# The modulation gates of a two-layer decoder trunk: summed along features like the shifts, then spread over the partitions through a row in DRAM

## The chip, the cores and the metric

The kernel runs on one core of a Trainium2 chip. The metric is device time in microseconds of the whole program, the median over runs; the version before has a median of 1032.69 us (three runs, 1031.07 to 1036.15).

## The reference

Two layers, batch 1, 256 tokens, model width 1024, float32 throughout. Each layer is a gated feed-forward block, a token mixer, and a second feed-forward block. All three are modulated by vectors that come from a conditioning vector `c`:

```python
c_act = jax.nn.silu(c)                                  # (1, 1024)
for l in range(2):
    mod = (c_act @ w_ada[l] + b_ada[l]).reshape(B, 3, 3, 1024)
    norm_mod = lambda h, j: rms(h) * g_norm[l, j] * (1 + mod[:, j, 1]) + mod[:, j, 0]
    gate     = lambda j: 1 + mod[:, j, 2]
    x = x + 0.5 * gate(0) * swiglu(norm_mod(x, 0), w_up[l, 0], w_down[l, 0])
    x = x +       gate(1) * mixer (norm_mod(x, 1), ...)
    x = x + 0.5 * gate(2) * swiglu(norm_mod(x, 2), w_up[l, 1], w_down[l, 1])
```

`w_ada` is 1024 x 9216 per layer: for each of the three blocks j a third for the shift, one for the scale, one for the gate. The six gates (two layers times three blocks) are what the change is about: each is a vector of 1024 numbers, and the kernel needs it as a tile of 128 partitions x 1024 in which every partition holds the same row, because it multiplies results that have tokens on the partitions and features along the free axis.

## The kernel before

**Matmuls.** Weights arrive from DRAM in units of 128 x 1024 floats (512 KB). `unit` loads one into a tile of the pool `raw` (6 buffers, line 255) and `split` (lines 248 and 249) makes two parts of it: ScalarE rounds it to fp32r (`H`), VectorE subtracts that from the original (`L`). The pool of these pairs has 11 buffers. Each product is three TensorE matmuls (H with the high part of the activations, L with it, H with their low part). A feed-forward block goes over 11 chunks of 256 hidden features: `up_w` (line 467) makes one half of a chunk for all 256 tokens from 4 units, `down` (lines 260 to 262) adds the product of one chunk to the output from 2 units. In steady order a chunk is: `up_w(j, 0)`, `down(j-1, 0)`, `up_w(j, 1)`, `down(j-1, 1)`.

**The modulation.** `w_ada` comes in the same 512 KB units through the same six `raw` buffers. A list `ada_todo` holds 11 stretches in a fixed order; the shift and scale of the very first block are done ahead of it. `ada_step(n)` takes the next n units off the list: after the second half of each chunk (`ADA_FFN`, 5 or fewer), and after each projection of the first layer's mixer (`ADA_MIX`). `ada_until` drains it where a result is needed.

- Shifts and scales (`ada_ss`): the unit is stored with 128 output features on the partitions and the 1024 inputs along the free axis. VectorE multiplies it with `cb`, the activated `c` on every partition, and adds up along the free axis (line 290, with an accumulator). One unit gives one column of 128 features; eight units give a 128 x 8 tile, feature k*128+p at partition p, column k.
- Gates (`ada_gate`): the unit is stored with inputs on the partitions and the 1024 outputs along the free axis. A tile `acc` (128 x 1024, pool `w4`) is set to zero by GpSimd (line 308) and its first row is loaded with the bias (line 309). For each of eight units VectorE adds unit times `cs[:, m]` (the activated `c`, one number a partition) to `acc` (line 313). After the eighth, `split(acc)` makes H and L of it, four TensorE matmuls of 512 columns with a matrix of ones (lines 321 and 322) sum over the partitions and put the sum on all 128 of them, and ScalarE copies the two halves from PSUM to the tile `gate`, with factor and offset 0.5 or 1 (line 323).

**Use of a gate.** `residual` (lines 441 and 442) multiplies a finished output with `gate` on VectorE and adds it to `x`. The tile `gate` has one buffer for block 1 and one shared by blocks 0 and 2; `gate_free` keeps a new gate from being begun before the last reader of its buffer has been emitted.

**Order.** All DMAs are issued by SyncE (SP), one after the other. The order of each engine's instructions is fixed when the program is built: a scheduler goes through the emitted instructions by priority (the order of emission) and lets a later one pass an earlier one that isn't ready by its model; on the chip each engine then keeps that order.

Of the kernel before, what the change touches and what calls it, by code (L numbers as in the profile page):

```python
# [9 lines left out]
F32 = mybir.dt.float32  # L10
# [3 lines left out]
AF = mybir.ActivationFunctionType  # L14
# [5 lines left out]
D = 1024  # L20
# [37 lines left out]
def ada_units():  # L58
    keys = []
    for l in range(DEPTH):  # L60
        for j in range(3):
            keys += [("ss", l, j, k, v) for k in range(KT) for v in range(2)]
            keys += [("gt", l, j, m) for m in range(KT)]
    return {k: i for i, k in enumerate(keys)}


# [7 lines left out]
def _offsets(sizes):  # L74
# [5 lines left out]


PAR, N_PAR = _offsets(
    [("c", KT), ("lam", 4 * DEPTH)]
    + [(f"{n}{l}{j}", KT) for l in range(DEPTH) for j in range(3) for n in ("bs", "bc", "gn")]
    + [(f"{n}{l}", k) for l in range(DEPTH)
       for n, k in (("cw", 16), ("cb", 4), ("br", 4), ("bi", 4), ("gm", 8), ("wf", 4 * KT))]
)
# [4 lines left out]


@with_exitstack
def trunk_kernel(ctx: ExitStack, tc: tile.TileContext, x, c, wst, ada, par, cst, row, bgate, wg, out):
    nc = tc.nc
    pool = lambda name, bufs, **k: ctx.enter_context(tc.tile_pool(name=name, bufs=bufs, **k))
    const = pool("const", 1)
# [11 lines left out]
    def W4(shape, dt=F32, name="w4"):  # L110
        return w4.tile(shape, dt, tag="w4", name=name)
# [48 lines left out]
    def P(name):  # L160
        o, n = PAR[name]
        return p_sb[:, o:o + n]
# [12 lines left out]
    RS = 0.5 * NEWTON ** 3  # L175


    cs = const.tile([128, KT], F32, name="cs")
    for n in range(2):
        q = slice(n * 512, (n + 1) * 512)  # L180
        o = PT([128, 512], name="pc")
        T.matmul(o, lhsT=one_row, rhs=c_row[:, q], start=True, stop=True)
        A.activation(cb[:, q], o, AF.Silu)
    A.activation(cs, P("c"), AF.Silu)

    V.tensor_scalar(out=P("gn00"), in0=P("gn00"), scalar1=RS, scalar2=None, op0=ALU.mult)
    V.scalar_tensor_tensor(out=P("bc00"), in0=P("bc00"), scalar=1.0, in1=P("gn00"), op0=ALU.add, op1=ALU.mult)
# [56 lines left out]
    def split(raw):  # L244
        h = hlp.tile([128, 1024], F32R, tag="H", name="H")
        lo = hlp.tile([128, 1024], F32R, tag="L", name="L")
        with held("A"):
            A.copy(h, raw)  # L248
        V.tensor_tensor(out=lo, in0=raw, in1=h.bitcast(F32), op=ALU.subtract)  # L249
        return h, lo  # L250
# [26 lines left out]

    ss_t = {}
    G_t, S_t, gate_t = {}, {}, {}
    acc_t = {}  # L280

    def ada_ss(l, j, k, v):
        if (k, v) == (0, 0):
            ss_t[l, j] = const.tile([128, 2, KT], F32, name=f"ss{l}{j}")
            G_t[l, j] = const.tile([128, KT], F32, name=f"G{l}{j}")
            S_t[l, j] = const.tile([128, KT], F32, name=f"S{l}{j}")
        raw = rawp.tile([128, D], F32, tag="raw", name="raw")
        S.dma_start(out=raw, in_=ada[A_UNITS["ss", l, j, k, v]])
        st = ss_t[l, j]
        V.scalar_tensor_tensor(out=raw, in0=raw, scalar=1.0, in1=cb,  # L290
                               op0=ALU.mult, op1=ALU.mult, accum_out=st[:, v, k:k + 1])
        first = (l, j) == (0, 0)
        if v == 1 and (first or k == KT - 1):
            q = slice(k, k + 1) if first else slice(0, KT)
            V.tensor_tensor(out=S_t[l, j][:, q], in0=st[:, 0, q], in1=P(f"bs{l}{j}")[:, q], op=ALU.add)
            if first:
                V.tensor_scalar(out=G_t[l, j][:, q], in0=st[:, 1, q], scalar1=P(f"gn{l}{j}")[:, q],
                                scalar2=P(f"bc{l}{j}")[:, q], op0=ALU.mult, op1=ALU.add)
                return
            V.scalar_tensor_tensor(out=G_t[l, j][:, q], in0=st[:, 1, q], scalar=1.0, in1=P(f"bc{l}{j}")[:, q],  # L300
                                   op0=ALU.add, op1=ALU.add)
            V.scalar_tensor_tensor(out=G_t[l, j][:, q], in0=G_t[l, j][:, q], scalar=RS, in1=P(f"gn{l}{j}")[:, q],
                                   op0=ALU.mult, op1=ALU.mult)

    def ada_gate(l, j, m):
        if m == 0:
            acc_t[l, j] = W4([128, D], name="acc")
            nc.gpsimd.memset(acc_t[l, j], 0.0)
            S.dma_start(out=acc_t[l, j][0:1, :], in_=bgate[l * 3 + j:l * 3 + j + 1, :])
        raw = rawp.tile([128, D], F32, tag="raw", name="raw")  # L310
        S.dma_start(out=raw, in_=ada[A_UNITS["gt", l, j, m]])
        acc = acc_t[l, j]
        V.scalar_tensor_tensor(out=acc, in0=raw, scalar=cs[:, m:m + 1], in1=acc, op0=ALU.mult, op1=ALU.add)
        if m == KT - 1:
            g = const.tile([128, D], F32, name=f"gate{j % 2}", tag=f"gate{j % 2}")
            f = 1.0 if j == 1 else 0.5
            h, lo = split(acc)
            for n in range(2):
                q = slice(n * 512, (n + 1) * 512)
                o = PT([128, 512], name="pg")  # L320
                T.matmul(o, lhsT=ones_r, rhs=h[:, q], start=True, stop=False)
                T.matmul(o, lhsT=ones_r, rhs=lo[:, q], start=False, stop=True)
                A.activation(g[:, n * 512:(n + 1) * 512], o, AF.Copy, scale=f, bias=f)
            gate_t[l, j] = g


# [635 lines left out]
def _pack(inp):  # L962
    f = lambda n: np.asarray(inp[n])
    up, dn, wi, wo, wa = f("w_ffn_up"), f("w_ffn_down"), f("w_in"), f("w_out"), f("w_ada")
    wst = np.empty((len(W_UNITS), 128, 1024), up.dtype)
    for key, i in W_UNITS.items():
        if key[0] == "up":
            _, l, s, j, h = key
            a = up[l, s].reshape(KT, 128, 2, FF)[2 * h:2 * h + 2, :, :, j * CH:(j + 1) * CH]
            wst[i] = a.transpose(1, 0, 2, 3).reshape(128, 1024)  # L970
        elif key[0] == "dn":
            _, l, s, j, h = key
            wst[i] = dn[l, s, j * CH + h * 128:j * CH + (h + 1) * 128]
        elif key[0] == "in":
            _, l, g, h = key
            a = np.concatenate([wi[l][:, lo:hi] for lo, hi in GROUP_COLS[g]], axis=1)
            wst[i] = a.reshape(KT, 128, 512)[2 * h:2 * h + 2].transpose(1, 0, 2).reshape(128, 1024)
        else:
            _, l, m = key
            wst[i] = wo[l, m * 128:(m + 1) * 128]  # L980
    ada = np.empty((len(A_UNITS), 128, 1024), wa.dtype)
    for key, i in A_UNITS.items():
        if key[0] == "ss":
            _, l, j, k, v = key
            ada[i] = wa[l].reshape(D, 3, 3, KT, 128)[:, j, v, k, :].T
        else:
            _, l, j, m = key
            ada[i] = wa[l].reshape(128, KT, 3, 3, D)[:, m, j, 2, :]

    par = np.zeros((128, N_PAR), np.float32)  # L990

    def put(name, a):
        o, n = PAR[name]
        par[:, o:o + n] = a

    cols = lambda v: v.reshape(-1, 128).T
    put("c", f("c").reshape(128, KT))
    put("lam", cols(f("lru_lambda")))
    ba = f("b_ada").reshape(DEPTH, 3, 3, D)
    for l in range(DEPTH):  # L1000
        for j in range(3):
            put(f"bs{l}{j}", cols(ba[l, j, 0]))
            put(f"bc{l}{j}", cols(ba[l, j, 1]))
            put(f"gn{l}{j}", cols(f("g_norm")[l, j]))
        put(f"cw{l}", cols(f("conv_w")[l]))
        put(f"cb{l}", cols(f("conv_b")[l]))
        put(f"br{l}", cols(f("b_rgate")[l]))
        put(f"bi{l}", cols(f("b_igate")[l]))
        put(f"gm{l}", cols(f("g_mix_out")[l]))
        put(f"wf{l}", wi[l][:, 2560:2564].reshape(KT, 128, 4).transpose(1, 0, 2).reshape(128, 4 * KT))  # L1010

    row = np.zeros((1, N_ROW), np.float32)
    for l in range(DEPTH):
        for n, a in (("bf", f("b_fgate")[l]), ("gqk", f("g_qk")[l].reshape(-1))):
            o, k = ROW[f"{n}{l}"]
            row[0, o:o + k] = a

    i = np.arange(128)
    le = i[:, None] <= i[None, :]
    consts = {  # L1020
        "ident": np.eye(128), "ntri": -1.0 * ~(i[:, None] < i[None, :]),
        "trif": le, "msb": np.where(i[:, None] < i[None, :], 0.0, -1e30),
        "mfx": np.where(i[None, :] <= i[:, None], 0.0, -1e30), "fold": i[:, None] % 4 == np.arange(4)[None, :],
    }
    cst = np.concatenate([consts[n] for n in CST], axis=1).astype(np.float32)

    wg = np.zeros((DEPTH, 128, 2, 4, 128), np.float32)
    for gi, n in enumerate(("w_rgate", "w_igate")):
        w = f(n).reshape(DEPTH, 4, 2, HD, HD)
        for b in range(2):  # L1030
            wg[:, b * HD:(b + 1) * HD, gi, :, b * HD:(b + 1) * HD] = w[:, :, b].transpose(0, 2, 1, 3)
    return {
        "x": f("x").reshape(SEQ, D), "c": f("c").reshape(1, D), "wst": wst, "ada": ada, "par": par, "cst": cst,
        "row": row, "bgate": np.ascontiguousarray(ba[:, :, 2].reshape(DEPTH * 3, D)), "wg": wg,
    }


# [15 lines left out]
```

## Time and profile before

| | |
|---|---|
| median of the runs | 1032.69 us |
| the profiled execution | 1031.17 us, span 1029.4 us |
| TensorE matmuls | 994.3 us busy, 97% of the span |
| VectorE | 759.9 us, 74% |
| ScalarE | 538.1 us, 52% |
| GpSimd | 53.3 us, 5% |
| DMA | 248.10 MB, mean 241 GB/s |
| mean granted TensorE clock | 0.994 |

The time of the profiled execution holds its span and 1.8 us around it. In the profile a row of a group reads: line, engine, operation, output <- inputs, shapes, count; then the busy time of the group in us and the mean of one instruction in ns; then how long the engine had been idle just before, and what ended that. PE is TensorE, PEld its weight loads, DVE VectorE, ACT ScalarE, POOL GpSimd, SPq the issuing of DMAs by SyncE. Matmuls overlap, so a matmul's own duration is longer than its step to the next one.

### The profile page before, as it was taken

How to read it: one execution, taken by the hardware profiler on the slowest of the kernel's cores; microseconds unless marked ns; L12 is line 12 of the kernel's file. 1: busy time of each engine (PE TensorE's matmuls, PEld its weight loads, DVE VectorE, ACT ScalarE, POOL GpSimd, SP SyncE). 2: the span in 40 equal slices, each digit the busy share in tenths (PEclk: the TensorE clock that was granted, in tenths of full speed). 3: DMA queues.
4: the chain of work that ended last, by engine and by line, in shares of the span. 5: the costliest groups of instructions: out<-in, count | busy, mean ns of one | idle time of the engine just before them, and what ended most of it. 6: DMA issues, size and time to landing. Idle time of an engine off the chain costs nothing.

```text
span 1029.4 us, 15807 instructions
## 1 busy us (share of the span) xinstructions
PE 994.3 (97%) x6038; PEld 871.8 (85%) x6038; DVE 759.9 (74%) x1107; ACT 538.1 (52%) x855; POOL 53.3 (5%) x108
## 2 busy tenths in 40 slices
PE   5999999989999899999999999999999989999998
PEld 4999999868787799999878999997777778999996
DVE  7988978769786898888569888665677559745452
ACT  5373534458774444354454455455679454635340
POOL 1000000120011200000020000001100120000000
PEclk9999999989999999999999999999999999999999
DMA  8989998757473699999539999853542328755511
GB/s 307 362 308 315 332 332 312 268 207 255 155 252 117 241 362 336 335 331 328 194 124 340 342 334 335 304 191 137 173 175 83 103 86 324 266 203 171 198 63 41
DMA packets 68922, 248.10 MB, mean 241 GB/s; under 512 B 7783, under 2 KB 8423, under 8 KB 68846
## 3 DMA queue, kind: packets, MB, share of 16 engines
q1 hardware_dynamic: 68846, 247.10, 68.2%
q8 instruction: 47, 0.77, 0.3%
q14 instruction: 29, 0.24, 0.1%
HBM read 246.02 MB, written 1.05 MB: 240 GB/s over the span
## 4 chain that ended last, share of the span: by engine, by line
PE 83%; ACT 6%; POOL 4%; DVE 3%; issue 2%; DMA 1%; SPq 0%; DVEq 0%; POOLq 0%; ACTq 0%
PE up L467 38%; PE dn L260 8%; PE dn L262 8%; PE dn L261 8%; PE up L271 5%; PE pj L271 5%; PE up L273 3%; PE pj L273 2%; ACT H L248 2%; POOL na L360 1%; PE wo L260 1%; PE wo L261 1%; PE wo L262 1%; POOL ny L361 1%; PE tp L415 1%
## 5 line engine op out<-in xcount | busy, mean ns | idle before, releaser
L249 DVE TENSOR_TENSOR L<-raw,H 128x1024 fp32r<-128x1024 f32 x320 | 380.5, 1221 | 72.6 <-ACT H L248 71.8
L248 ACT CAST H<-raw 128x1024 fp32r<-128x1024 f32 x320 | 328.1, 1051 | 84.5 <-PE up L467 35.0
L467 PE MATMUL up<-hTh,H 128*128 128x256 f32 x1088 | 211.0, 282 | 3.7 <-ACT H L248 3.7
L467 PE MATMUL up<-hTl,H 128*128 128x256 f32 x1088 | 211.9, 283 | 0.0
L467 PE MATMUL up<-hTh,L 128*128 128x256 f32 x1088 | 211.3, 282 | 0.0
L467 PEld LDWEIGHTS up<-hTh,H 128*128 128x128 f32 x1088 | 169.2, 189 | 9.9 <-ACT H L248 4.1
L467 PEld LDWEIGHTS up<-hTl,H 128*128 128x128 f32 x1088 | 165.1, 189 | 0.0
L467 PEld LDWEIGHTS up<-hTh,L 128*128 128x128 f32 x1088 | 164.4, 189 | 0.0
L459 ACT ACTIVATE sg<-up 128x256 f32<-128x256 f32 x88 | 33.7, 383 | 223.9 <-PE up L467 183.6
L260 PE MATMUL dn<-H,gh 128*128 128x512 f32 x352 | 141.1, 401 | 1.6 <-ACT gh L532 1.6
L262 PE MATMUL dn<-H,gl 128*128 128x512 f32 x352 | 140.0, 399 | 0.0
L261 PE MATMUL dn<-L,gh 128*128 128x512 f32 x352 | 139.7, 397 | 0.0
L290 DVE SCALAR_TENSOR_TENSOR raw<-raw,cb 128x1024 f32<-128x1024 f32 x96 | 114.0, 1220 | 2.1 <-DMA raw<-in_ada 2.1
L262 PEld LDWEIGHTS dn<-H,gl 128*128 128x128 f32 x352 | 66.6, 189 | 15.8 <-DVE gl L533 0.5
L260 PEld LDWEIGHTS dn<-H,gh 128*128 128x128 f32 x352 | 66.7, 189 | 15.2 <-ACT gh L532 3.0
L261 PEld LDWEIGHTS dn<-L,gh 128*128 128x128 f32 x352 | 66.9, 190 | 12.8
L516 DVE TENSOR_TENSOR sg<-sg,up 128x256 f32<-128x256 f32 x68 | 28.5, 419 | 66.0 <-ACT sg L459 65.7
L271 PE MATMUL pj<-H,hTh 128*128 128x512 f32 x160 | 66.2, 414 | 0.0
L273 PE MATMUL pj<-H,hTl 128*128 128x512 f32 x160 | 65.9, 412 | 0.0
L271 PE MATMUL up<-H,hTh 128*128 128x512 f32 x160 | 64.2, 401 | 0.4 <-DVE hTh L428 0.4
L271 PE MATMUL pj<-L,hTh 128*128 128x512 f32 x160 | 64.5, 403 | 0.0
L271 PE MATMUL up<-L,hTh 128*128 128x512 f32 x160 | 63.1, 395 | 0.0
(249 smaller groups left out, 1101.5 us busy)
## 6 DMA issues: line engine op xcount, KB each, us to landing
raw<-in_wst SPq DMA_DIRECT2D x320, 512.0 KB, 5.2
raw<-in_ada SPq DMA_DIRECT2D x144, 512.0 KB, 5.3
x<-in_x SPq DMA_DIRECT2D x2, 512.0 KB, 3.7
wgt<-in_wg SPq DMA_DIRECT2D x2, 512.0 KB
out_x<-x SPq DMA_DIRECT2D x4, 256.0 KB
once<-in_cst SPq DMA_DIRECT2D x1, 192.0 KB
p_sb<-in_par SPq DMA_DIRECT2D x1, 148.0 KB, 5.4
r_sb<-in_row SPq DMA_DIRECT2D x1, 132.0 KB, 6.1
```

Of the source, the lines that this page charges most:

```text
L248: A.copy(h, raw)
L249: V.tensor_tensor(out=lo, in0=raw, in1=h.bitcast(F32), op=ALU.subtract)
L260: T.matmul(o, lhsT=xh, rhs=wh, start=first, stop=False)
L261: T.matmul(o, lhsT=xh, rhs=wl, start=False, stop=False)
L262: return T.matmul(o, lhsT=xl, rhs=wh, start=False, stop=last)
L271: T.matmul(o, lhsT=hh[:, k, :], rhs=part, start=k == 0 and i == 0, stop=False)
L273: mul = T.matmul(o, lhsT=hl[:, k, :], rhs=w(k)[0], start=False, stop=k == KT - 1)
L290: V.scalar_tensor_tensor(out=raw, in0=raw, scalar=1.0, in1=cb, op0=ALU.mult, op1=ALU.mult, accum_out=st[:, v, k:k + 1])
L360: E.tensor_scalar(out=a, in0=y, scalar1=v, scalar2=y, op0=ALU.mult, op1=ALU.mult)
L459: used.append(A.activation(*a, **k))
L467: return T.matmul(o[:, v], lhsT=w[:, q:q + 128], rhs=(hTh, hTl)[h][:, :, k, :], start=opens, stop=True, skip_group_check=True)
L516: V.tensor_tensor(out=sg, in0=sg, in1=o[:, 1], op=ALU.mult)
```

## The change

The gates are computed as the shifts are. The gate units are stored in the layout of the shift units, and VectorE makes one column of 128 features from each, with `cb`. After the eighth unit two small VectorE instructions on 128 x 8 add the bias (now a part of the table of parameters `par`, `bg`) and apply `(1 + v) * f`. Then SP stores the 128 x 8 tile to a row of 1024 floats in DRAM, feature k*128+p at its place, and loads that row into all 128 partitions of `gate`. `acc`, its zeroing, the bias load, `cs`, the split, the four matmuls and the two copies go. The tiles `ss` of the shifts and scales now share two buffers.

```diff
-    + [(f"{n}{l}{j}", KT) ... for n in ("bs", "bc", "gn")]
+    + [(f"{n}{l}{j}", KT) ... for n in ("bs", "bc", "bg", "gn")]
...
-    A.activation(cs, P("c"), AF.Silu)
...
-            ss_t[l, j] = const.tile([128, 2, KT], F32, name=f"ss{l}{j}")
+            ss_t[l, j] = const.tile([128, 2, KT], F32, name=f"ss{l}{j}", tag=f"ss{(3 * l + j) % 2}")
...
-    def ada_gate(l, j, m):
-        if m == 0:
-            acc_t[l, j] = W4([128, D], name="acc")
-            nc.gpsimd.memset(acc_t[l, j], 0.0)
-            S.dma_start(out=acc_t[l, j][0:1, :], in_=bgate[l * 3 + j:l * 3 + j + 1, :])
+    rows = pool("rows", 2, space=bass.MemoryType.DRAM)
+
+    def ada_gate(l, j, k):
+
+        if k == 0:
+            gt_t[l, j] = const.tile([128, KT], F32, name=f"gt{l}{j}", tag=f"gt{j % 2}")
         raw = rawp.tile([128, D], F32, tag="raw", name="raw")
-        S.dma_start(out=raw, in_=ada[A_UNITS["gt", l, j, m]])
-        acc = acc_t[l, j]
-        V.scalar_tensor_tensor(out=acc, in0=raw, scalar=cs[:, m:m + 1], in1=acc, op0=ALU.mult, op1=ALU.add)
-        if m == KT - 1:
+        S.dma_start(out=raw, in_=ada[A_UNITS["gt", l, j, k]])
+        col = gt_t[l, j]
+        V.scalar_tensor_tensor(out=raw, in0=raw, scalar=1.0, in1=cb, op0=ALU.mult, op1=ALU.mult,
+                               accum_out=col[:, k:k + 1])
+        if k == KT - 1:
+            f = 1.0 if j == 1 else 0.5
+            V.tensor_tensor(out=col, in0=col, in1=P(f"bg{l}{j}"), op=ALU.add)
+            V.tensor_scalar(out=col, in0=col, scalar1=1.0, scalar2=f, op0=ALU.add, op1=ALU.mult)
+            r = rows.tile([1, D], F32, tag="row", name="row")
+            S.dma_start(out=r.rearrange("o (k p) -> p (o k)", p=128), in_=col)
             g = const.tile([128, D], F32, name=f"gate{j % 2}", tag=f"gate{j % 2}")
-            f = 1.0 if j == 1 else 0.5
-            h, lo = split(acc)
-            for n in range(2):
-                q = slice(n * 512, (n + 1) * 512)
-                o = PT([128, 512], name="pg")
-                T.matmul(o, lhsT=ones_r, rhs=h[:, q], start=True, stop=False)
-                T.matmul(o, lhsT=ones_r, rhs=lo[:, q], start=False, stop=True)
-                A.activation(g[:, n * 512:(n + 1) * 512], o, AF.Copy, scale=f, bias=f)
+            S.dma_start(out=g, in_=r.broadcast_to([128, D]))
             gate_t[l, j] = g
```

More of the change, by code (lines that the diff above doesn't have):

```diff
@@ L62, in ada_units @@
             keys += [("ss", l, j, k, v) for k in range(KT) for v in range(2)]
-            keys += [("gt", l, j, m) for m in range(KT)]
+            keys += [("gt", l, j, k) for k in range(KT)]
     return {k: i for i, k in enumerate(keys)}
@@ L82 @@
 PAR, N_PAR = _offsets(
-    [("c", KT), ("lam", 4 * DEPTH)]
-    + [(f"{n}{l}{j}", KT) for l in range(DEPTH) for j in range(3) for n in ("bs", "bc", "gn")]
+    [("lam", 4 * DEPTH)]
+    + [(f"{n}{l}{j}", KT) for l in range(DEPTH) for j in range(3) for n in ("bs", "bc", "bg", "gn")]
     + [(f"{n}{l}", k) for l in range(DEPTH)
@@ L94, in trunk_kernel @@
 @with_exitstack
-def trunk_kernel(ctx: ExitStack, tc: tile.TileContext, x, c, wst, ada, par, cst, row, bgate, wg, out):
+def trunk_kernel(ctx: ExitStack, tc: tile.TileContext, x, c, wst, ada, par, cst, row, wg, out):
     nc = tc.nc
@@ L175, in trunk_kernel @@
     RS = 0.5 * NEWTON ** 3
-    cs = const.tile([128, KT], F32, name="cs")
     for n in range(2):
@@ L279, in trunk_kernel @@
     G_t, S_t, gate_t = {}, {}, {}
-    acc_t = {}
+    gt_t = {}
     def ada_ss(l, j, k, v):
         if (k, v) == (0, 0):
-            ss_t[l, j] = const.tile([128, 2, KT], F32, name=f"ss{l}{j}")
+            ss_t[l, j] = const.tile([128, 2, KT], F32, name=f"ss{l}{j}", tag=f"ss{(3 * l + j) % 2}")
             G_t[l, j] = const.tile([128, KT], F32, name=f"G{l}{j}")
@@ L986, in _pack @@
         else:
-            _, l, j, m = key
-            ada[i] = wa[l].reshape(128, KT, 3, 3, D)[:, m, j, 2, :]
+            _, l, j, k = key
+            ada[i] = wa[l].reshape(D, 3, 3, KT, 128)[:, j, 2, k, :].T
     par = np.zeros((128, N_PAR), np.float32)
@@ L996, in _pack @@
     cols = lambda v: v.reshape(-1, 128).T
-    put("c", f("c").reshape(128, KT))
     put("lam", cols(f("lru_lambda")))
@@ L1003, in _pack @@
             put(f"bc{l}{j}", cols(ba[l, j, 1]))
+            put(f"bg{l}{j}", cols(ba[l, j, 2]))
             put(f"gn{l}{j}", cols(f("g_norm")[l, j]))
@@ L1033, in _pack @@
         "x": f("x").reshape(SEQ, D), "c": f("c").reshape(1, D), "wst": wst, "ada": ada, "par": par, "cst": cst,
-        "row": row, "bgate": np.ascontiguousarray(ba[:, :, 2].reshape(DEPTH * 3, D)), "wg": wg,
+        "row": row, "wg": wg,
     }
```

## The prediction

> **What bounds the kernel now.** I read first how the engines are filled over stretches of time. Columns after the stretch: its length, then busy us of PE, PEld, DVE, ACT and POOL with counts, the granted PE clock, the DMA share and GB/s.
>
> ```profile
> 100.00:150.00 50.00, 50.00 (x358) 46.95 (x357) 42.53 (x55) 22.49 (x33) 0.00 (x0) 1.00 0.94 333
> 200.00:250.00 50.00, 45.16 (x195) 35.69 (x194) 40.10 (x58) 34.48 (x52) 9.71 (x11) 0.93 0.67 231
> 400.00:475.00 75.00, 75.00 (x531) 70.17 (x530) 61.17 (x89) 34.57 (x47) 0.00 (x0) 1.00 0.94 335
> 520.00:600.00 80.00, 78.36 (x475) 69.23 (x474) 71.28 (x90) 41.65 (x65) 5.47 (x8) 1.00 0.80 283
> ```
>
> In the feed-forward blocks (first and third row) TensorE has no gap at all: 50.00 of 50 and 75.00 of 75 us. But the DMA engines are 94% busy there and VectorE 85% (42.53 of 50): two others are close behind. Only around the mixer (second row) does TensorE idle, 4.8 us of 50, and its clock falls with it to 0.93.
>
> Next, in the timeline of PE, what the old spreading of a gate costs there; this is the first gate (the last two rows are for later).
>
> ```profile
> 114.36 0.39 PE L321 MATMUL pg<-H,ones_r 128*128 128x512 f32 x1
> 114.59 0.39 PE L322 MATMUL pg<-L,ones_r 128*128 128x512 f32 x1
> 114.82 0.39 PE L321 MATMUL pg<-H,ones_r 128*128 128x512 f32 x1
> 115.05 0.39 PE L322 MATMUL pg<-L,ones_r 128*128 128x512 f32 x1
> 115.28 0.39 PE L260 MATMUL dn<-H,gh 128*128 128x512 f32 x1
> ...
> 118.08 0.40 PE L467 MATMUL up<-hTh,H 128*128 128x256 f32 x2
> ...
> 125.16 0.40 PE L260 MATMUL dn<-H,gh 128*128 128x512 f32 x1
> ```
>
> Each matmul lasts 0.39 us, but the next begins 0.23 us after it: the four hold TensorE for 115.28 - 114.36 = 0.92 us, with real work right behind. The group of these matmuls over the whole program:
>
> ```profile
> L322 PE MATMUL pg<-L,ones_r x12: 392/392/581, 114.6 to 880.0; 128*128 128x512 f32 x12
> its engine sat idle before it (us, times) until:
> who waited for it (us, times):
> ```
>
> Twelve here and as many for line 321. Under neither of the two headings stands an entry: TensorE never waited for the split, and nobody for the sum. What they cost is their place in the queue of the engine that bounds the kernel.
>
> **The change part by part.**
>
> *TensorE.* 24 matmuls go, at a step of 0.23 us: 24 x 0.23 = 5.5 us; nothing is added. With no idle time around them, in five of six gates everything behind moves up by that. In the second gate, which is made in the mixer, TensorE is 45.16 of 50 us busy, so a tenth of its 0.9 us may be lost in a gap. I take 5.5 us.
>
> *VectorE, ScalarE, GpSimd.* The old tile `acc`, and then the shift's form of the sum, which the new gate takes over:
>
> ```profile
> L313 DVE SCALAR_TENSOR_TENSOR acc<-raw,cs,acc x48: 1275/1284/1287, 79.1 to 868.5; 128x1024 f32<-128x1024 f32 x48
> L308 POOL MEMSET acc<- x6: 951/951/977, 8.7 to 843.3; 128x1024 f32 x6
> L309 SPq DMA_DIRECT2D acc<-in_bgate x6: 243/244/281, 68.8 to 844.3; - x6
> L248 ACT CAST H<-acc x6: 1047/1048/1051, 105.2 to 869.8; 128x1024 fp32r<-128x1024 f32 x6
> L249 DVE TENSOR_TENSOR L<-acc,H x6: 1218/1226/1227, 106.3 to 870.9; 128x1024 fp32r<-128x1024 f32 x6
> its engine sat idle before it (us, times) until:
>   DVE acc L313: 26.8, 5
> ```
>
> ```profile
> L290 DVE SCALAR_TENSOR_TENSOR raw<-raw,cb x96: 1211/1220/1227, 11.7 to 662.1; 128x1024 f32<-128x1024 f32 x96
> L290 DVE DVE_READ_ACCUMULATOR raw<-raw,cb x96: 78/83/89, 12.9 to 663.2; 128x1 f32 x96
> ```
>
> A gate costs VectorE 8 x (1.220 + 0.083 - 1.284) = +0.15 us for the sums, -1.23 us for the low part, and two new instructions on 128 x 8. Those lie between the 0.083 us of a 128 x 1 read and the 1.22 us of 128 x 1024; at their size nearer the first, I take 0.2 us each. That is -0.7 us a gate, 4 us in all. ScalarE loses six casts of 1.05 us, twelve copies and, worth more, the 26.8 us in which it stood before the cast of `acc` with everything else queued behind. None of that was on TensorE's path, so it is costed at nothing; at most it moves weights forward. GpSimd's six clearings (0.95 us) are off the path too. A pair H and L of the eleven is no longer taken by `acc`.
>
> *The way through DRAM.* A gate must be ready when the residual multiplies with it:
>
> ```profile
> L441 DVE TENSOR_TENSOR tmp<-dn,gate x16: 682/690/694, 197.6 to 1024.9; 128x512 f32<-128x512 f32 x16
> L323 ACT ACTIVATE gate<-pg x12: 592/601/612, 115.8 to 880.5; 128x512 f32<-128x512 f32 x12
> ```
>
> The first gate is made at 115.8 us and first used at 197.6. Eighty us cover two DMAs many times over, so their latency is free; without that cover it would be the store's and the load's landing, some 10 us a gate. What isn't free is the queue they stand in. All loads of weights go through SP:
>
> ```profile
> 101.38 7.98 SPq L255 DMA_DIRECT2D raw<-in_wst  x6
> 110.55 6.95 SPq L288 DMA_DIRECT2D raw<-in_ada  x5
> ```
>
> The store waits for the second small VectorE instruction, 0.4 us after the sum that also frees the next `raw` buffer, so at this point SP would have had little else to issue. The load back waits until the store has landed, and behind it wait loads of weights that could start when a `raw` buffer comes free. How long a landing takes:
>
> ```profile
> q1 hardware_dynamic: 68846, 247.10, 68.2%
> ...
> raw<-in_ada SPq DMA_DIRECT2D x144, 512.0 KB, 5.3
> ...
> r_sb<-in_row SPq DMA_DIRECT2D x1, 132.0 KB, 6.1
> ```
>
> ```profile
> SPq L1049 <- DMA out_x<-x: 1.6, 2, 1.4
> ```
>
> With other loads ahead of it, 5.3 us for 512 KB and 6.1 us for a short row spread to all partitions, which is just the kind of load that is added; for a store with nothing ahead, SP waited 1.4 us at the very end. The store is peculiar: feature k*128+p of partition p lies 512 bytes from its next, so 128 x 8 values are 1024 separate pieces of 4 bytes, 64 for each of 16 DMA engines. No row shows such a transfer. Bounds: nothing beyond an ordinary landing; or every piece as dear as the mean packet of the profile, 0.682 x 16 x 1029.4 us / 68846 = 163 ns, which is 64 x 0.163 = 10.4 us. A mean packet carries 3.6 KB (247.10 MB / 68846), a thousand times a piece, so I take a value near the low end, 1 us.
>
> The Trainium skill speaks against the change here: in "DMA: Bandwidth & Descriptors", Rules for kernel authors, a strided last dimension lowers to one descriptor per element and should be rearranged; under Specifications, below 512 bytes the engine does a read-modify-write. It gives no price per piece; by it the time would lie towards the upper bound, and the sum below would end as in the rival that is slower.
>
> So SP may stand for up to 5.3 + 1 = 6.3 us a gate, less what the scheduler has put between store and load. The load adds 512 KB at 333 GB/s, 1.6 us. What hides this is the lead of the weights over TensorE; in the timeline of DVE after the first gate:
>
> ```profile
> 101.27 3.92 DVE L313 SCALAR_TENSOR_TENSOR acc<-raw,cs,acc 128x1024 f32<-128x1024 f32 x3
> ...
> 109.29 4.63 DVE L249 TENSOR_TENSOR L<-raw,H 128x1024 fp32r<-128x1024 f32 x4
> ...
> 118.68 1.22 DVE L249 TENSOR_TENSOR L<-raw,H 128x1024 fp32r<-128x1024 f32 x1
> ```
>
> The four units at 109.29 are the next chunk's. The first is ready at 110.5 and used at 118.08: a lead of 7.6 us. The unit at 118.68 is the second of a `down`, ready at 119.9, used at 125.16: 5.3 us, the smallest. A stand of 6.3 us that begins with the queue still holding several loads eats the lead, but hardly more. I cost it at 0; the ends are -2 us (a pair and VectorE time more for the weights) and +10.4 us a gate (dear pieces, below). Lost lead can be regained: VectorE has 15% of the time free.
>
> *The rest.* `par` grows by 40 columns, 20 KB or 0.06 us at 333 GB/s; the activation for `cs` goes; `ss` shares two buffers, each read out before the next but one begins. Nothing for these.
>
> Sum: -5.5 us. The profiled execution's 1031.17 us (its span 1029.4 and 1.8 around it) would become 1025.7. The median of the runs is 1.5 us higher, 1032.69, so 1027.2 us.
>
> **The rivals.**
>
> *The gain is given back.* DMA (94%) and VectorE (85%) take over as soon as TensorE is faster, or the lead that is lost at a gate is paid for by small waits. For it: a chunk of 17 us has 16 us of DMA, and the added load makes 17.6 in one chunk. Against it: TensorE has not one gap there now. It leaves 1029 to 1033, I say 1031.
>
> *Slower: SP stands longer than the lead.* Place: the four gates in stretches with full DMA (first, third, fourth, fifth). Price: stand less 5.3 us, each time. It decides from 5.3 us on; slower by 0.5% (5.2 us) it gets when the four lose 5.5 + 5.2 = 10.7 us, so at a stand of 8.0 us. At the upper bound, 5.3 + 10.4 = 15.7 us, TensorE loses 4 x 10.4 = 42 us: 1069. At half that price a piece, 4 x 5.2 - 5.5 = +15: 1048, which I name. For it: 1024 pieces; against it: their few bytes, and loads still on their way.
>
> *More is gained.* ScalarE's 26.8 us and the free pair let weights come earlier where TensorE does wait, in the 1.6 us idle of 520 to 600 and the 4.8 of 200 to 250: up to 4 us more, 1023.
>
> **How the numbers follow.** The forecast has 0.50, its own range 1024.5 to 1029.5; given back 0.25; slower 0.13; more 0.12. A measurement can tell about 0.5%, 5.2 us, from no change: faster is below 1027.5. That holds for two thirds of the forecast (its small errors lean to the gain) and for "more": 0.34 + 0.12 = 0.46. Same: 0.16 and 0.22 of "given back", 0.38. Slower: 0.03 and 0.13, 0.16. The range 1022 to 1037 leaves out the dear part of "slower" and a little of "more".
>
> **What would show it.** Right: no row `pg`; `dn` 0.23 us after `up` at that place; PE busy about 5 us lower and still 50.00 of 50 in the first stretch; SP's wait for the store under 6 us. Wrong: waits of PE or PEld for `H` or `L` within 20 us of a gate, SP waiting over 8 us on the row's store, a clock under 1.00 in the feed-forward blocks.

## The result and the profile after

The changed kernel takes 1072.87 us (median of four runs, 1069.66 to 1074.85) against 1033.09 us beside it: 1.038 times as long, interval 1.034 to 1.042. The forecast was 1027.2 us.

The page of the changed kernel: busy time of the engines, and the two new DMAs in the list of issues (KB each, median us from issue to landing, which is when the transfer is reported complete).

```profile
PE 1005.9 (94%) x6014; PEld 876.5 (82%) x6014; DVE 750.4 (70%) x1161; ACT 530.3 (49%) x836; POOL 49.8 (5%) x102
...
gate<-row SPq DMA_DIRECT2D x6, 512.0 KB, 6.6
```

```profile
row<-gt SPq DMA_DIRECT2D x6, 4.0 KB, 13.1
```

The 24 matmuls are gone (6014 in place of 6038), and yet PE is busy 11.6 us longer. The span is 1073.1 us, so PE is idle 67.2 us, where it was 1029.4 - 994.3 = 35.1 before. Idle 32.1 more and busy 11.6 more make the 43.7 us between the two spans. And the store of 4 KB, the smallest transfer of the change, takes 13.1 us to land. That figure is the median of the two stores, of six, whose landing the trace could tell; SP issues the load that waits for the store 10.9 to 14.0 us after it, with a median of 12.2.

What each engine does in the 20 us that follow each of the six stores (PE, PEld, DVE, ACT, POOL; then PE clock, DMA share, GB/s):

```profile
101.70:121.70 20.00, 18.55 (x130) 16.85 (x128) 6.71 (x9) 3.89 (x6) 0.00 (x0) 1.00 0.53 148
238.30:258.30 20.00, 12.44 (x56) 9.61 (x54) 8.96 (x11) 8.34 (x12) 0.00 (x0) 0.90 0.72 151
383.30:403.30 20.00, 17.40 (x113) 15.90 (x113) 5.91 (x9) 4.11 (x7) 0.00 (x0) 0.94 0.53 148
580.70:600.70 20.00, 16.19 (x107) 14.75 (x106) 5.82 (x8) 4.50 (x7) 0.00 (x0) 0.96 0.64 115
624.40:644.40 20.00, 10.21 (x65) 9.03 (x64) 5.32 (x8) 2.50 (x3) 0.00 (x0) 0.80 0.55 125
907.70:927.70 20.00, 20.00 (x141) 18.36 (x139) 6.96 (x9) 4.78 (x7) 0.00 (x0) 1.00 0.48 130
```

The kernel before, in the 20 us after its second and its fifth gate's sum:

```profile
232.00:252.00 20.00, 20.00 (x90) 16.21 (x89) 18.86 (x29) 17.61 (x26) 0.00 (x0) 1.00 0.84 288
605.00:625.00 20.00, 20.00 (x136) 18.38 (x136) 15.91 (x24) 9.04 (x14) 0.00 (x0) 1.00 0.98 339
```

Where 288 to 362 GB/s flowed at the six places before, 115 to 151 do; VectorE works 5 to 9 us of 20 because it has no data. TensorE falls from full work to 10.2 of 20 us at the fifth store and to 12.4 at the second, the one in the mixer. After the sixth it still lives on its lead, and pays a little later: in the timeline of PE it waits 3.75 us, and then its matmuls step by 0.42 to 0.59 us, soon by a steady 0.43, in place of 0.23 (the first two rows), while the granted clock is 0.50 (the row of a stretch below).

```profile
927.16 0.39 PE L259 MATMUL dn<-L,gh 128*128 128x512 f32 x1
927.39 0.40 PE L260 MATMUL dn<-H,gl 128*128 128x512 f32 x1
931.54 0.79 PE L258 MATMUL dn<-H,gh 128*128 128x512 f32 x1 [3.75 <-ACT gh L518]
932.13 0.63 PE L259 MATMUL dn<-L,gh 128*128 128x512 f32 x1
932.58 0.79 PE L260 MATMUL dn<-H,gl 128*128 128x512 f32 x1
933.17 0.63 PE L258 MATMUL dn<-H,gh 128*128 128x512 f32 x1
933.59 0.63 PE L259 MATMUL dn<-L,gh 128*128 128x512 f32 x1
934.02 0.63 PE L260 MATMUL dn<-H,gl 128*128 128x512 f32 x1
```

```profile
934.00:936.50 2.50, 2.50 (x12) 2.38 (x11) 2.50 (x3) 1.89 (x3) 0.00 (x0) 0.50 0.84 316
```

That is how PE can be busier with fewer matmuls: the mean granted clock fell from 0.994 to 0.975.

The first store closer, as SP issues it and as the DMA engines then move data (last two columns: share, GB/s):

```profile
101.72 0.39 SPq L319 DMA_DIRECT2D row<-gt  x1
102.16 1.05 SPq L253 DMA_DIRECT2D raw<-in_wst  x2
112.65 0.33 SPq L321 DMA_DIRECT2D gate<-row  x1
113.03 1.92 SPq L253 DMA_DIRECT2D raw<-in_wst  x3
```

```profile
101.00:103.00 2.00, 2.00 (x19) 2.00 (x18) 1.93 (x7) 0.00 (x0) 0.00 (x0) 1.00 0.20 30
103.00:105.00 2.00, 2.00 (x15) 1.83 (x14) 1.22 (x3) 0.66 (x2) 0.00 (x0) 1.00 0.11 1
105.00:107.00 2.00, 2.00 (x11) 1.63 (x10) 1.48 (x3) 0.96 (x2) 0.00 (x0) 1.00 0.18 14
107.00:109.00 2.00, 2.00 (x20) 2.00 (x19) 0.25 (x1) 0.00 (x0) 0.00 (x0) 1.00 0.32 37
109.00:111.00 2.00, 2.00 (x20) 2.00 (x19) 0.00 (x0) 0.00 (x0) 0.00 (x0) 1.00 0.25 23
111.00:113.00 2.00, 2.00 (x18) 1.92 (x17) 0.00 (x0) 0.00 (x0) 0.00 (x0) 1.00 0.60 29
```

Two things happen. SP stands from 103.2 to 112.65 us before the load of the gate. In the list of SP's waits (us in total, times, longest) this wait has 11.1 us a time, for the four stores for which the trace names it:

```profile
SPq L321 <- DMA row<-gt: 44.5, 4, 12.4
```

And the two loads of weights that it had issued right behind the store don't come either: from 101 to 113 us 1 to 37 GB/s flow. ScalarE, in its timeline, waits for just these:

```profile
116.41 1.05 ACT L246 CAST H<-raw 128x1024 fp32r<-128x1024 f32 x1 [10.45 <-DMA raw<-in_wst]
```

The trace also records each packet that the DMA engines move. The 1024 pieces themselves are quick: by this record they take 7 to 9 ns each, and the last of them has passed 1.6 us after the first store's issue. The packets of 4096 bytes behind them, which carry weights, are slow: up to 6.9 us each in this kernel, where their median is 0.159 us. So the time goes by between the pieces' passing and the store's landing, and not in handling one piece after another.

### The profile page after: what moved, and what is told of

Its sections match the earlier page's. It is cut to its first block, busy times and chain, and to the rows that moved or that the text cites. A ratio compares the mean times of both kernels' runs of the same rounds, so it can differ in the third digit from the quotient of the medians.

```text
span 1073.1 us, 15747 instructions
## 1 busy us (share of the span) xinstructions
PE 1005.9 (94%) x6014; PEld 876.5 (82%) x6014; DVE 750.4 (70%) x1161; ACT 530.3 (49%) x836; POOL 49.8 (5%) x102
## 4 chain that ended last, share of the span: by engine, by line
PE 55%; issue 23%; DMA 7%; ACT 6%; DVE 5%; POOL 4%; SPq 0%; POOLq 0%; ACTq 0%; DVEq 0%
PE up L465 23%; PE dn L258 5%; PE dn L259 5%; PE dn L260 5%; DMA raw<-in_wst 5%; PE pj L269 4%; PE up L269 3%; ACT H L246 2%; PE pj L271 2%; PE up L271 2%; POOL na L358 1%; DVE raw L312 1%; DMA row<-gt 1%; DVE L L247 1%; PE wo L258 1%
## 5 line engine op out<-in xcount | busy, mean ns | idle before, releaser
L465 PE MATMUL up<-hTh,H 128*128 128x256 f32 x1088 | 213.4, 284 | 18.8 <-ACT H L246 18.8
```

The lines of the kernel that those rows point to most:

```text
L465: return T.matmul(o[:, v], lhsT=w[:, q:q + 128], rhs=(hTh, hTl)[h][:, :, k, :], start=opens, stop=True, skip_group_check=True)
```

## The experiments

Two theories. P: the 1024 pieces of the store hold up the DMA engines, whoever waits for it. Q: the price is SP standing in front of the load of the gate, with the weights queued behind. Where pieces are concerned two more, N and C, come below.

**The store without anyone waiting for it.**

```diff
-            S.dma_start(out=g, in_=r.broadcast_to([128, D]))
+            S.dma_start(out=g, in_=c.broadcast_to([128, D]))
```

> Left out: the gate tile is loaded from the vector c, not from the stored row, so the numbers of the gates are not those of the reference; the store of 1024 pieces stays, but nothing waits for it. Theory P (the pieces themselves hold up the DMA engines for some 12 us, whoever waits): SP issues its loads at once, but they land some 12 us late all the same, about 1060 to 1073 us. Theory Q (the price is SP standing before the load of the gate, with the weights queued behind it): without the wait at most 1032 us. Near 1050 both hold a part.

1056.87 us, 1.024 times the time before (1.022 to 1.025): between the two. The wait accounts for 1072.87 - 1056.87 = 16 us; the larger part stays although SP is free. In the 16 us lies one thing more: as nothing ties the load of the gate to the store now, it is issued elsewhere, the first at 91.50 us, ahead of the store at 100.72. The 20 us after the first store:

```profile
100.70:120.70 20.00, 18.52 (x131) 16.86 (x130) 8.12 (x11) 6.27 (x8) 0.00 (x0) 1.00 0.77 183
```

183 GB/s, with six loads of weights issued at once behind the store.

**Neither store nor wait.**

```diff
-            S.dma_start(out=r.rearrange("o (k p) -> p (o k)", p=128), in_=col)
-            S.dma_start(out=g, in_=r.broadcast_to([128, D]))
+            S.dma_start(out=g, in_=c.broadcast_to([128, D]))
```

> Left out: the store; the gate tile is loaded from the vector c, so its numbers are not those of the reference. What is left is the change without its way through DRAM, with the same 512 KB load. Both theories: the sum of the prediction without any stand of SP, 1027 us (1024 to 1031). If it is over 1035, something else than the store made the change slow (the sums, the load of the gate, the new order of the engines).

1024.78 us, 0.9925 of the time before (0.991 to 0.994). So the sums in the new form, the bias, and a 512 KB load into all partitions cost nothing and the gain is there; the store alone, with nobody waiting, costs 1056.87 - 1024.78 = 32 us. That is the larger part of what the change lost, and it is theory P's.

**Pieces of 32 bytes.** The host packs the gate's units so that column k of partition p is feature 8p + k.

```diff
-            S.dma_start(out=r.rearrange("o (k p) -> p (o k)", p=128), in_=col)
+            S.dma_start(out=r.rearrange("o (p k) -> p (o k)", p=128), in_=col)
...
-            ada[i] = wa[l].reshape(D, 3, 3, KT, 128)[:, j, 2, k, :].T
+            ada[i] = wa[l].reshape(D, 3, 3, 128, KT)[:, j, 2, :, k].T
...
-            put(f"bg{l}{j}", cols(ba[l, j, 2]))
+            put(f"bg{l}{j}", ba[l, j, 2].reshape(128, KT))
```

> The gate units are packed so that partition p holds features 8p to 8p+7: the store becomes 128 pieces of 32 bytes in place of 1024 of 4, with the same wait and the same load. Theory P: an eighth of the pieces, 1.6 us in place of 13; the store lands some 5 us after its issue, within the lead of the weights, 1027 to 1034 us. Theory Q in the form that any round trip through DRAM behind full queues is too long: little changes, over 1050 us.

1024.45 us, 0.9922 of the time before (0.9903 to 0.994): the version that beats both kernels, with the same wait and the same round trip through DRAM. The store's row and its landing, then the first and the second gate's 20 us:

```profile
L319 SPq DMA_DIRECT2D row<-gt x6: 326/327/330, 101.9 to 864.1; - x6
...
DMA to landing us min/median/max: 1.4/1.4/3.0
```

```profile
101.90:121.90 20.00, 20.00 (x146) 18.79 (x145) 15.54 (x23) 7.74 (x11) 0.00 (x0) 1.00 0.88 332
232.00:252.00 20.00, 19.89 (x87) 15.44 (x86) 17.69 (x26) 17.21 (x28) 0.00 (x0) 1.00 0.90 292
```

Landed after 1.4 us in place of 13.1, and faster as a whole than either theory said; TensorE has no gap at the first gate and none worth the name at the second. Q in the form that any round trip is too long has fallen.

**Both DMAs on GpSimd's queue**, with the 1024 pieces as they were.

```diff
-            S.dma_start(out=r.rearrange("o (k p) -> p (o k)", p=128), in_=col)
+            nc.gpsimd.dma_start(out=r.rearrange("o (k p) -> p (o k)", p=128), in_=col)
...
-            S.dma_start(out=g, in_=r.broadcast_to([128, D]))
+            nc.gpsimd.dma_start(out=g, in_=r.broadcast_to([128, D]))
```

> Both new DMAs (the store of 1024 pieces and the load of the gate) are issued by GpSimd; SP carries only the loads of weights and never stands for the row. Theory P: the pieces run on the same DMA engines and hold up the weights there, 1055 to 1073 us. Theory Q: about 1027 us.

1033.67 us, 1.001 times the time before (0.9998 to 1.0023). Neither theory as written. The store is as slow as ever:

```profile
L319 POOL DMA_DIRECT2D row<-gt x6: 906/967/1098, 101.8 to 874.1; - x6
...
DMA to landing us min/median/max: 9.3/10.7/12.5
```

```profile
101.80:121.80 20.00, 20.00 (x145) 18.75 (x144) 13.29 (x19) 7.58 (x11) 1.68 (x2) 1.00 0.95 266
107.80:113.80 6.00, 6.00 (x47) 5.74 (x47) 2.66 (x3) 0.81 (x1) 0.58 (x1) 1.00 0.73 67
230.00:250.00 20.00, 14.24 (x58) 11.19 (x57) 11.25 (x13) 11.41 (x14) 1.51 (x2) 0.84 0.64 201
```

266 GB/s flow in the 20 us after the first store, where the same pieces in SP's own queue left 183. But the weights don't simply go past the store. They flow on until the pieces reach the DMA engines, at the first store 2.5 to 4.5 us after the issue by the packets' record; then, in the 6 us of the second row, 67 GB/s flow although every load of weights is in SP's queue. Each of the other five stores has such a stretch of 6 us, with 42 to 107 GB/s; in the last run below, with pieces of 32 bytes, the same stretch after the first store has 306. So P holds in part whichever queue the store is in: the other queue shortens the hold-up, it doesn't end it. What it still costs is 1033.67 less the 1024.12 us of that last run, 9.6 us, and the mixer's gate is the clearest place: 14.24 us of work in 20, where the last run has 18.19. Why the hold-up is shorter isn't settled. The queue is one difference; another is that GpSimd's store goes out as 16 packets of 256 bytes, where SP's goes out as 1024 of 4, and a store of 1024 packets from a second queue was not run.

**What makes a piece dear.** Theory C: each costs its DMA engine about 0.19 us (12 us / 64). Theory N: small writes close together hold each other up. In the next run the pieces are as many and as small, but 64 bytes apart.

```diff
-            r = rows.tile([1, D], F32, tag="row", name="row")
-            S.dma_start(out=r.rearrange("o (k p) -> p (o k)", p=128), in_=col)
+            r = rows.tile([1, D * 16], F32, tag="row", name="row")
+            S.dma_start(out=r.rearrange("o (k p s) -> p (o k) s", p=128, s=16)[:, :, 0:1], in_=col.unsqueeze(2))
...
-            S.dma_start(out=g, in_=r.broadcast_to([128, D]))
+            S.dma_start(out=g, in_=c.broadcast_to([128, D]))
```

> As the run with the store that nobody waits for, but each of the 1024 pieces of 4 bytes goes to a place of its own 64 bytes apart (a row of 64 KB in place of 4 KB); left out as there: the gate tile is loaded from c. Theory N (neighbouring small writes into the same few bytes hold each other up): the store lands in about 2 us, and the time goes to 1025 to 1030 us. Theory C (each piece costs its DMA engine about 0.19 us wherever it goes): as there, a landing near 11 us and 1052 to 1060 us.

1024.95 us, and a landing of 3.2 us:

```profile
L319 SPq DMA_DIRECT2D row<-gt x6: 377/377/387, 101.1 to 862.1; - x6
...
DMA to landing us min/median/max: 2.8/3.2/5.1
```

32 us are gone by nothing but distance. C has fallen, and with it the count as the main price. The packets' record says the same: here too nearly all pieces take 7 to 9 ns each, but the weights' packets behind them take 2.4 us at most.

Pairs of 8 bytes and quads of 16, in the change's row, wait and load as there (the packing goes along, as with 32 bytes):

```diff
-            S.dma_start(out=r.rearrange("o (k p) -> p (o k)", p=128), in_=col)
+            S.dma_start(out=r.rearrange("o (q p m) -> p (o q) m", p=128, m=2), in_=col.rearrange("p (q m) -> p q m", m=2))
```

> Gate units packed so that a partition's 8 values lie in 4 pairs: the store is 512 pieces of 8 bytes, wait and load as in the change. Theory C (price by the count): 32 pieces an engine in place of 64, landing 6 to 7 us in place of 13; the stand is about as long as the lead of the weights, so 1024 to 1035 us. If the price went by bytes alone, the landing would stay at 13 us and the time at 1073.

1029.13 us, 0.9965 of before (0.9947 to 0.9983); landing 4.6 us, less than the 6 to 7 of theory C.

> The same with 256 pieces of 16 bytes. Theory C: landing 3 to 4 us, time as with 128 pieces, 1022 to 1028 us.

1025.9 us (one time); landing 3.7 us, as C said for this one; the run doesn't tell C from N.

Two more with 1024 pieces of 4 bytes. First 16 bytes apart (`s=4` and a row of `D * 4` in the diff above):

> As the spread store, but the 1024 pieces of 4 bytes lie 16 bytes apart (a row of 16 KB); left out as there: the gate tile is loaded from c. If the price goes with the number of pieces in the same 64 bytes (16 in the change, 1 in the spread run), four share them here as with the 256 pieces of 16 bytes, so a landing near 4 us and about 1026 us. If any neighbours nearer than 64 bytes are as bad as in the change, landing near 11 us and about 1056 us.

1025.43 us, landing 4.0 us. Then 8 bytes apart, but with all pieces of 64 bytes from one partition:

```diff
-            r = rows.tile([1, D * 16], F32, tag="row", name="row")
-            S.dma_start(out=r.rearrange("o (k p s) -> p (o k) s", p=128, s=16)[:, :, 0:1], in_=col.unsqueeze(2))
+            r = rows.tile([1, D * 4], F32, tag="row", name="row")
+            S.dma_start(out=r.rearrange("o (p k s) -> p (o k) s", p=128, s=2)[:, 0:KT, 0:1], in_=col.unsqueeze(2))
```

> 1024 pieces of 4 bytes, eight of them in each 64 bytes (8 bytes apart), but all eight from the same partition; the next partition begins 128 bytes on. Left out as before: the gate tile is loaded from c. If it is pieces of different partitions in the same 64 bytes that hold each other up, a landing near 3 us as in the spread run and about 1025 us. If the number of pieces in the same 64 bytes decides, whoever writes them, half the landing of the change's store, 5 to 7 us, and 1025 to 1035 us.

1028.25 us, landing 5.3 us. That pieces of different partitions disturb each other isn't borne out; the number close together is. In one table, median landings (of two stores in the change, of five in the others; the next DMA waits for the store in the rows marked w):

| pieces | in each 64 bytes | in each 32 bytes | landing, us |
|---|---|---|---|
| 1024 of 4 bytes, the change (w) | 16 | 8 | 13.1 |
| the same, not waited for | 16 | 8 | 10.8 |
| 1024 of 4 bytes, 8 bytes apart | 8 | 4 | 5.3 |
| 512 of 8 bytes (w) | 8 | 4 | 4.6 |
| 1024 of 4 bytes, 16 bytes apart | 4 | 2 | 4.0 |
| 256 of 16 bytes (w) | 4 | 2 | 3.7 |
| 1024 of 4 bytes, 64 bytes apart | 1 | 1 | 3.2 |
| 128 of 32 bytes (w) | 2 | 1 | 1.4 |

Rows with the same number in 64 bytes lie together, whether there are 256 or 1024 pieces; the count adds a smaller part (1.4 against 3.2). Counted in 32 bytes they lie together as well, so the table doesn't tell the unit. Nor does it set a price for waiting: the single stores of the first row, by SP's rows, took 10.9 to 14.0 us, those of the second 9.2 to 12.5.

**The first term of the sum by itself**: the kernel before, with each gate's four matmuls done twice.

```diff
+                T.matmul(o, lhsT=ones_r, rhs=h[:, q], start=True, stop=False)
+                T.matmul(o, lhsT=ones_r, rhs=lo[:, q], start=False, stop=True)
                 T.matmul(o, lhsT=ones_r, rhs=h[:, q], start=True, stop=False)
                 T.matmul(o, lhsT=ones_r, rhs=lo[:, q], start=False, stop=True)
```

> The kernel before, with the four matmuls that spread a gate done twice (24 more matmuls of 512 columns, the same result). The prediction's first term says that they stand on the path at 0.23 us each: 5.5 us slower, 1038 us. If TensorE had slack there, no change (1031 to 1034 us).

1038.34 us against 1032.73, 1.0057 times (1.0039 to 1.0076): 5.6 us for 24 matmuls.

**32 bytes and GpSimd's queue together.**

> 128 pieces of 32 bytes, with the store and the load of the gate issued by GpSimd, so that SP never stands for the row. If SP's short stand in the run with 32 bytes still costs something, a few us less than there (1018 to 1022); if the lead of the weights hides it, the same 1024 us.

1024.12 us, 0.9919 of before (0.9887 to 0.995): the same as from SP's queue. A short stand is hidden. From GpSimd the store lands after 4.9 us, from SP after 1.4, and that is hidden too.

## Why the prediction was wrong

*TensorE, 5.5 us:* right. Twice the matmuls cost 5.6 us, and in the kernel without a store PE is busy 988.8 us, 5.5 less than before.

*VectorE and the rest:* right in kind, off the path as said. VectorE is busy 9.5 us less (750.4 after 759.9), where the sum had 4. The two small instructions last 0.166 and 0.169 us where 0.2 was taken, the load of the gate lands in 6.6 us (6.1 was the nearest row), and without the dear store the kernel is 6 to 9 us faster than before (0.9925, 0.991 to 0.994), a little more than the sum said.

*The store, 1 us: the step that failed.* It was put on top of an ordinary landing, 5.3 + 1 = 6.3 us, and the stores of the 1024 pieces landed after 9.2 to 14.0; with 32-byte pieces a store lands after 1.4, so the small pieces cost about 10 us where 1 was taken. The bounds held that (5.3 + 10.4 = 15.7 at the dear end); the choice within them went by bytes, "a thousand times a piece". Bytes don't set it. Nor does the upper end's reasoning hold, the price of a mean packet, 163 ns, for each of 1024 pieces: a piece passes in 7 to 9 ns, and the same number 64 bytes apart land in 3.2 us. The range failed with the choice, since I gave the dear half only the small chance of the rival.

*"SP may stand": a second step, its effect.* I counted only loads that SP couldn't issue. The two that it had issued behind the store stood as well: 16 us go with the wait, 32 with the store. The mechanism "Slower" named the right transfer, and its 1069 us at the upper bound are near the 1072.87; that agreement is luck, because it counted four gates, only SP's stand, and no clock. At the 11.1 us that SP did stand, the same formula gives 4 x (11.1 - 5.3) - 5.5 = +18, about 1050. The runs show loss at all six, the most at the fifth, 44 us after the fourth, probably because the lead hadn't been regained, and at the second, in the mixer, where it hadn't been counted at all. SP also stands ahead of each store until the small VectorE instruction is done, 23.2 us over the six; with 32-byte pieces that is 22.8 us, and as that kernel is fast, it is hidden.

*The clock* I named only as a sign of being wrong. It is a term: PE is 11.6 us busier with 5.5 us less to do, so 17 us are slower steps; the granted clock of the whole fell to 0.975, where the kernel without the store has 0.993.

The Trainium skill's rule from "DMA: Bandwidth & Descriptors", Rules for kernel authors, that a strided last dimension is to be rearranged, would have forecast the sign, and rearranging is what mended it. The trace bears out the advice but not the count of descriptors as the main reason. By the same page of the Trainium skill, Queues, rings and completion order, an engine takes the descriptors of a ring in order and goes round robin between rings. The trace agrees in part: 183 GB/s flow behind the store in one queue and 266 beside it from another, but there too the loads are held for some 6 us at 42 to 107 GB/s.

*Rivals.* "Given back" fell: in the runs without the dear store TensorE keeps its gain. "More is gained" got a part: 1024.45 us with 32 bytes.

## What to carry to other kernels

Before a small store into DRAM is costed by its bytes, count how many separate pieces it writes close together (within each 64 bytes, say; the unit isn't known); if the host can permute the data so that a partition's values lie side by side, do that first, as it turned 1.038 into 0.992 here. A DMA that may be slow doesn't belong in the queue that feeds the engine that bounds the kernel: the loads issued behind it are late even when nothing waits for it. Another queue makes that milder but doesn't cure it (1033.67 us here, against 1024.12 with wider pieces). And compare a stand with the smallest lead of all stretches, with the time that the lead needs to come back.

## What the runs showed of the hardware

- 4 KB in 1024 pieces of 4 bytes, side by side in DRAM, land after 9.2 to 14.0 us; the same pieces 64 bytes apart 3.2, 8 in each 64 bytes 5.3, 4 in each 4.0, and 128 pieces of 32 bytes 1.4. Whether the unit is 64 bytes, 32 or another one, and whether bytes in DRAM or the pieces' order within an engine make it, stays open: the rows also differ in length, 4 to 64 KB, and only distances of 4, 8, 16 and 64 bytes were tried.
- The DMA engines take such pieces in 7 to 9 ns each, and packets of 4096 bytes that come after them last up to 7 us in place of 0.159. When the store goes through GpSimd's queue, loads in SP's queue are held as well: some 6 us at 42 to 107 GB/s at each store.
- One row of 4 KB read into all 128 partitions lands like any load of 512 KB: 5.8 us in the kernel with 32 bytes, where a weight's takes 5.3 there.
- A gap of 3.75 us in TensorE was followed by some 5 us of matmuls at about 0.43 us a step in place of 0.23, with a granted clock of 0.50.
